# Attention projections 512 columns wide, and the next group's projection between the head pairs

## The chip, the core and the metric

The kernel runs on one core of one Trainium2 chip. The metric is device time in microseconds (us). The engines are named as in the profile: PE is TensorE (matrix products; PEld is its loading of the stationary operand), DVE is VectorE, ACT is ScalarE, POOL is GpSimd, and SP is SyncE, whose queue issues most transfers.

## The reference

The program is one inference step of a two-layer encoder trunk for 640 tokens: a prompt of 512 and 8 running streams of 16. Layer 0 is a mixer (spatial gating and a gated convolution) and a feed-forward block; layer 1 is forgetting attention and a feed-forward block. The change is in the attention. Cut to it:

```
z = rmsnorm(x) @ w_in                        # 1024 -> 3 x 1024 + 16
q, k, v, f = split(z)                        # 16 heads of 64
q, k = rmsnorm(q, q_norm), rmsnorm(k, k_norm)       # per head
logf = log_sigmoid(f + b_f);  d = cumsum(logf)
s = q k^T / 8 + d_query - d_key,  later keys masked
o = softmax(s) v                             # streams: 256 cached keys ahead of their own 16
x = x + o @ w_out;   k, v and logf are outputs too
```

All of it is float32. The kernel splits each float32 operand into two float32r parts (hi and lo) and forms hi x hi, lo x hi and hi x lo, so a product of the reference is three matrix products here.

## The kernel before

Tokens are in five blocks of 128, the last of which holds the streams; the 1024 features are eight chunks (h[0] to h[7], each a hi and a lo tile: hh, hl). The 16 heads are four groups of four heads, and a group is two pairs of heads.

**Projection.** `project` (L484 to L524) makes queries, keys and values of one group, one kind after the other. A kind is 256 columns wide. Its weights come as two tiles of 128 x 1024 from DRAM, by `weights` (L77): a landing tile `raw`, and `whi` and `wlo`, which ACT (L88) and DVE (L89) write. All three have three buffers. For each block of tokens 8 chunks x 3 products go into half a PSUM bank of `pj` (two banks); the activations are stationary and 256 columns of the weights move (L507). ACT evacuates each block (L510); for queries and keys ACT squares (L515), DVE sums by head (L516), POOL takes the root (L152), and DVE multiplies (L519, L521 for the keys). Keys and values leave for DRAM on ACT's queue (L523).

**Attention of a group.** `stream_operands` (L597; its transposes are L602) transposes the streams' queries and keys. `operands` (L529) builds the operands of a pair: transposes on PE (L537), evacuated and split by ACT and DVE (L544 to L549), with parts copied to other partitions by transfers on SP's queue (qa to qa, L545; ka to kb, L548; decay sums from DRAM, L551 and L552). `prompt_block` takes 128 queries of one head: two products for the scores (L569, L570) into one of two `sc` banks, mask and maximum on DVE, exponential on ACT, reciprocal and scaling on DVE, transposes of the probabilities (L576), evacuation to `u` (L579, L581), and the product with the values (L583, `pv`). `streams_pair` does the same for two streams (L634 to L670).

**Order.** The loop at L743 says for each group: project, then operands of the first pair, then for each pair the steps "b30", "s0", "b31", "o", ... where b30 is block 3 of head 0 of the pair, s0 is a stream step, and "o" in the first pair makes the second pair's operands. The tile framework then orders each engine's instructions by a schedule of its own, in which an instruction that comes earlier in the program goes first where both can run. So products of the next group's projection stand between the attention products of the present one. The decay sums (`decay`, L413) are made between queries and keys of group 0: forget logits (`pf`), their logarithms, running sums, and a way through DRAM. Behind group 3, the output projection over the chunks of groups 0 to 2 (`po`, L764 to L774, using the `pj` banks) is what remains to stand between.

## Time and profile before

| | us |
|---|---|
| time, median of 3 runs | 1533.71 (1533.48 to 1533.86) |
| profiled execution, span from the first to the last instruction | 1531.9 |
| PE busy in it | 1517.8 |
| DVE busy | 899.1 |
| ACT busy | 559.4 |
| POOL busy | 237.4 |

The profiled execution has no time of its own beside its span; the median of the runs is 1.8 us longer than the span. A busy time is the sum over which an engine had an instruction under way; products on PE overlap, so their spacing is read from the chain of waits, which gives, in order of time, pieces of "start, length, engine, tile, line, count". In the groups of instructions, "x480 | 137.7, 287" means 480 instructions, 137.7 us busy, 287 ns from start to end of one. A timeline row is "start, length, engine, line, operation, out<-in".

### The profile page before, as it was taken

Reading aid. Unit: us, or ns where it says so; the run is one execution under the profiler, and the core shown is the slowest. Engines: PE = TensorE matmul, PEld = TensorE weight load, DVE = VectorE, ACT = ScalarE, POOL = GpSimd, SP = SyncE. Lnnn points to the kernel's source line nnn. Section 1 sums busy time; section 2 is a strip of 40 time slices with the busy share of each in tenths; the row PEclk is TensorE's granted clock in tenths of the full one; section 3 lists DMA queues with packets and bytes.
Section 4 is the critical chain, followed back from the end, with each engine's and each line's share of the span. In section 5 each row is a group of like instructions: output and inputs, shape, how many; then the busy total and the mean of one; then the engine's idle time right before and its main releaser. Section 6 shows DMA issues by size and latency. Waiting matters only on the chain.

```text
span 1531.9 us, 26648 instructions
## 1 busy us (share of the span) xinstructions
PE 1517.8 (99%) x11008; PEld 1473.5 (96%) x11008; DVE 899.1 (59%) x1541; ACT 559.4 (37%) x918; POOL 237.4 (15%) x281
## 2 busy tenths in 40 slices
PE   8999999999999999999999999999999999999999
PEld 6999999999999999999989888888999999999998
DVE  6545437644653655675676766768765466365463
ACT  5422334322322322345545454535432233133231
POOL 5000122201210201143111111003221021021010
PEclk9999999999999999999999999999999999999999
DMA  6222212222223222243544343523222222321313
GB/s 226 77 82 73 77 56 85 68 81 85 62 64 95 64 66 93 62 156 103 180 128 136 122 123 104 183 60 107 83 60 76 87 67 57 98 73 53 107 47 106
DMA packets 52296, 142.90 MB, mean 93 GB/s; under 512 B 6656, under 2 KB 13744, under 8 KB 52048
## 3 DMA queue, kind: packets, MB, share of 16 engines
q1 hardware_dynamic: 45424, 133.79, 28.6%
q10 hardware_dynamic: 6752, 7.41, 1.4%
q8 instruction: 87, 1.43, 0.4%
q14 instruction: 33, 0.27, 0.1%
HBM read 125.41 MB, written 11.54 MB: 89 GB/s over the span
## 4 chain that ended last, share of the span: by engine, by line
PE 96%; DVE 2%; issue 1%; ACT 1%; DMA 0%; POOL 0%; SPq 0%; DVEq 0%; ACTq 0%
PE mm L109 71%; PE pj L507 10%; PE pv L583 3%; PE po L109 2%; PE pt L576 1%; PE mm L239 1%; PE pt L662 1%; PE sc L569 1%; DVE hl L132 1%; PE sc L570 1%; DVE wlo L89 1%; PE scs L641 1%; PE pt L537 1%; PE pt L655 0%; PE scs L634 0%
## 5 line engine op out<-in xcount | busy, mean ns | idle before, releaser
L88 ACT CAST whi<-raw 128x1024 fp32r<-128x1024 f32 (+4 forms) x222 | 207.6, 937 | 494.6 <-PE mm L109 426.1
L109 PE MATMUL mm<-hl,whi 128*128 128x320 f32 x1664 | 379.4, 309 | 0.5 <-DVE hl L132 0.5
L109 PE MATMUL mm<-hh,whi 128*128 128x320 f32 x1664 | 379.8, 309 | 0.0
L109 PE MATMUL mm<-hh,wlo 128*128 128x320 f32 x1664 | 379.2, 309 | 0.0
L109 PEld LDWEIGHTS mm<-hl,whi 128*128 128x128 f32 x1664 | 278.2, 188 | 0.7 <-DVE hl L132 0.7
L109 PEld LDWEIGHTS mm<-hh,whi 128*128 128x128 f32 x1664 | 278.2, 188 | 0.1
L109 PEld LDWEIGHTS mm<-hh,wlo 128*128 128x128 f32 x1664 | 278.0, 188 | 0.0
L89 DVE TENSOR_TENSOR wlo<-raw,whi 128x1024 fp32r<-128x1024 f32 (+4 forms) x222 | 245.5, 1107 | 33.3 <-ACT whi L88 33.0
L109 PE MATMUL mm<-sh,wlo 128*128 128x320 f32 x866 | 197.2, 309 | 1.3 <-DVE wlo L89 1.3
L109 PE MATMUL mm<-sl,whi 128*128 128x320 f32 x866 | 197.2, 309 | 0.0
L109 PE MATMUL mm<-sh,whi 128*128 128x320 f32 x866 | 196.2, 309 | 0.0
L202 POOL COPY so<-zp 128x18 f32<-128x18 f32 x88 | 89.4, 1016 | 570.4 <-DVE zp L191 570.4
L190 DVE TENSOR_TENSOR zp<-mm,rb 128x512 f32<-128x512 f32 x88 | 60.9, 692 | 195.8 <-PE mm L109 195.8
L209 DVE TENSOR_TENSOR x<-mm,x 128x640 f32<-128x640 f32 x79 | 65.0, 823 | 185.6 <-PE mm L109 185.6
L198 DVE SCALAR_TENSOR_TENSOR t<-zp,cst,t 128x656 f32<-128x656 f32 x184 | 165.1, 900 | 10.3 <-ACT t L196 5.6
L109 PEld LDWEIGHTS mm<-sh,wlo 128*128 128x128 f32 x866 | 144.6, 188 | 1.6 <-DVE wlo L89 1.6
L109 PEld LDWEIGHTS mm<-sl,whi 128*128 128x128 f32 x866 | 144.8, 188 | 0.0
L109 PEld LDWEIGHTS mm<-sh,whi 128*128 128x128 f32 x866 | 144.4, 188 | 0.2 <-issue 0.2
L507 PE MATMUL pj<-wlo,hh 128*128 128x256 f32 x480 | 137.7, 287 | 0.7 <-DVE wlo L89 0.7
L507 PE MATMUL pj<-whi,hh 128*128 128x256 f32 x480 | 137.7, 287 | 0.0
L507 PE MATMUL pj<-whi,hl 128*128 128x256 f32 x480 | 137.5, 287 | 0.0
L507 PEld LDWEIGHTS pj<-wlo,hh 128*128 128x128 f32 x480 | 91.6, 191 | 2.8 <-issue 1.6
(188 smaller groups left out, 1691.3 us busy)
## 6 DMA issues: line engine op xcount, KB each, us to landing
raw<-w_up SPq DMA_DIRECT2D x88, 512.0 KB
raw<-w_dn SPq DMA_DIRECT2D x32, 384.0 KB
raw<-w_c SPq DMA_DIRECT2D x24, 512.0 KB
raw<-w_dn SPq DMA_DIRECT2D x32, 320.0 KB
raw<-w_ab SPq DMA_DIRECT2D x16, 512.0 KB
ck<-c_k SPq DMA_DIRECT2D x16, 512.0 KB
cv<-c_v SPq DMA_DIRECT2D x16, 512.0 KB
o_kv<-z ACTq DMA_DIRECT2D x8, 640.0 KB
```

Of the source, the lines that this page charges most:

```text
L88: nc.scalar.copy(out=hi[:, c], in_=raw[:, c])
L89: nc.vector.tensor_tensor(out=lo[:, c], in0=raw[:, c], in1=hi[:, c].bitcast(F32), op=ALU.subtract)
L109: nc.tensor.matmul(outs[h], lhsT=l, rhs=r[:, h * HT:(h + 1) * HT], start=start and k == 0, stop=stop and k == 2)
L132: nc.vector.scalar_tensor_tensor(out=lo, in0=x, scalar=gs, in1=hi.bitcast(F32), op0=ALU.mult, op1=ALU.subtract)
L190: nc.vector.tensor_tensor(out=op, in0=a[:, 0:TP], in1=b[:, 0:TP], op=ALU.mult)
L198: nc.vector.scalar_tensor_tensor(out=cv[:, 0:CW], in0=zp[:, i:i + CW], scalar=w[:, i:i + 1], in1=cv[:, 0:CW], op0=ALU.mult, op1=ALU.add)
L202: self.nc.gpsimd.tensor_copy(out=out.rearrange("p (s c) -> p s c", c=2), in_=zp[:, 496:ZW].rearrange("p (s c) -> p s c", c=18)[:, :, 16:18])
L209: self.nc.vector.tensor_tensor(out=x, in0=ps[:, C0:C0 + T], in1=x, op=ALU.add)
L239: nc.tensor.matmul(pvs[tb], lhsT=l[:, tb * P:(tb + 1) * P], rhs=r[:, (kc % 2) * 512:(kc % 2 + 1) * 512], start=kc == 0 and k == 0, stop=kc ...
L507: nc.tensor.matmul(out[tb], lhsT=l[:, tb * P:(tb + 1) * P], rhs=r[:, c:c + 256], start=kc == 0 and i == 0, stop=kc == 7 and i == 2)
L537: nc.tensor.transpose(t[:, tb * P:(tb + 1) * P], z[i][:, tb, pair * P:(pair + 1) * P], k.ident)
L583: nc.tensor.matmul(ov[64 * hh:64 * hh + 64, i * P:n], lhsT=z[2][:, j, (2 * pair + hh) * 64:(2 * pair + hh) * 64 + 64], rhs=u[:, j * P:(j + ...
```

## The change

The weights of queries and keys of a group stand side by side in DRAM (`w_qk`, 512 columns), and so do the values of two groups (`w_vc`). `project` is replaced by `walk`, `project_qk` (one group) and `project_v` (two groups). Each product is 512 columns wide and fills a whole `pj` bank; a projection holds four weight tiles, and a block of tokens is evacuated, squared and normed when its walk is done. `whi` and `wlo` have four buffers, `raw` keeps three. In group 0 the queries and keys are projected, then the decay sums are made, then the values of groups 0 and 1 are projected. Queries and keys of group g+1 are projected at step "o" of the first pair of group g; the values of groups 2 and 3 at step "o" of the second pair of group 0. The remaining lines of the diff take comments out, lay out the weights in DRAM, and set a smaller scratch area for transfers that this kernel doesn't issue.

```diff
-        self.wp = pool(ctx, "wts", bufs=3)
+        self.wp = pool(ctx, "wts", bufs=4)
...
-        raw = self.wp.tile([P, 1024], F32, tag="raw", name=self.nm("raw"))
+        raw = self.wp.tile([P, 1024], F32, tag="raw", name=self.nm("raw"), bufs=3)
...
-    def project(self, g, h, first, after_q=None):
...
+    def walk(self, us, n, h, pairs):
+
+        k, nc = self.k, self.nc
+        out = [None] * 5
+        for tbs in ([(0, 1), (2, 3), (4,)] if pairs else [(tb,) for tb in range(5)]):
+            for tb in tbs:
+                out[tb] = self.pj.tile([P, 512], F32, tag="pj", name=k.nm("pj"))
+            for kc in range(8):
+                wh, wl = us[kc // n]
+                hh, hl = h[kc]
+                c = (kc % n) * 512
+                for tb in tbs:
+                    for i, (l, r) in enumerate(((hh, wh), (hl, wh), (hh, wl))):
+                        nc.tensor.matmul(out[tb], lhsT=l[:, tb * P:(tb + 1) * P], rhs=r[:, c:c + 512],
+                                         start=kc == 0 and i == 0, stop=kc == 7 and i == 2)
+            for tb in tbs:
+                yield tb, out[tb]
+
+    def project_qk(self, g, h):
+
+        k, nc, io = self.k, self.nc, self.io
+        us = [k.weights(io["w_qk"][g, u]) for u in range(4)]
+        zt = self.zp.tile([P, 5, 512], F32, tag="qk", name=k.nm("z"), bufs=2)
+        ss = self.zp.tile([P, 40], F32, tag="ss", name=k.nm("ss"))
+        for tb, o in self.walk(us, 2, h, g == 0):
+            nc.scalar.activation(out=zt[:, tb, :], in_=o, func=AF.Copy, scale=self.rt[:, tb:tb + 1])
+            sq = self.zp.tile([P, 512], F32, tag="sq", name=k.nm("sq"), bufs=1)
+            nc.scalar.activation(out=sq, in_=zt[:, tb, :], func=AF.Square)
+            s = ss[:, tb * 8:tb * 8 + 8]
+            nc.vector.reduce_sum(out=s, in_=sq.rearrange("p (h d) -> p h d", d=64), axis=AX.X)
+            k.rstd_of(s, s, 1.0 / 64)
...
+    def project_v(self, gg, h):
+
+        k, nc, io = self.k, self.nc, self.io
+        us = [k.weights(io["w_vc"][gg, u]) for u in range(4)]
+        zt = self.zp.tile([P, 5, 512], F32, tag="v", name=k.nm("z"), bufs=2)
+        for tb, o in self.walk(us, 2, h, False):
+            nc.scalar.activation(out=zt[:, tb, :], in_=o, func=AF.Copy, scale=self.rt[:, tb:tb + 1])
...
+    qk, v = at.project_qk(0, h), []
+    decay()
+    v += at.project_v(0, h)
     for g in range(4):
-        z = at.project(g, h, g == 0, decay if g == 0 else None)
+        z = qk + (v[g],)
...
                 if st == "o":
                     if pair == 0:
                         pops[1] = at.operands(g, 1, z)
+                        if g < 3:
+                            qk = at.project_qk(g + 1, h)
+                    elif g == 0:
+                        v += at.project_v(1, h)
```

The schedule follows. In the rows below a row is an instruction on PE in its order: line, operation, out<-in, size, and a count where equal ones follow each other. z are the projected queries, keys or values, pt a PSUM tile of transposes, p and u probabilities before and after their transposition, pp and pn those of the streams, on the streams' results, ka, kb, qa and qb the operands of a pair. Lines of the new kernel are six higher in the attention (L543 is the transpose of the operands, L575 and L576 are the scores).

The start of group 2 on PE, before: the operands' transposes, with the last products of the group ahead between them, and then products of the projection.

```order
L583 MATMUL pv_8406<-u_8636,z_7941 64x128
L537 MATMUL pt_9153<-cst,z_8668 128x128
L583 MATMUL pv_8406<-u_8652,z_7941 64x128
L537 MATMUL pt_9153<-cst,z_8668 128x128 x3
L537 MATMUL pt_9158<-cst,z_8836 128x128 x4
L507 MATMUL pj_9734<-whi_9728,hl_6173 128x256
L507 MATMUL pj_9734<-wlo_9729,hh_6172 128x256
```

The same place in the change:

```order
L543 MATMUL pt_8601<-cst,z_8009 128x128 x4
L589 MATMUL pv_8334<-u_8580,z_6742 64x128
L543 MATMUL pt_8606<-cst,z_8009 128x128 x4
L109 MATMUL po_9976<-sh_9373,whi_9971 128x320
L109 MATMUL po_9977<-sh_9373,whi_9971 128x320
L575 MATMUL sc_8636<-ka_8612,qa_8611 128x512
L640 MATMUL scs_8662<-sr,sl 128x272
```

Before, a run of projection products followed the transposes; now two products of the output projection stand between the transposes and the first score.

The second pair of group 2 on PE, before:

```order
L583 MATMUL pv_9187<-u_9329,z_9006 64x128 x3
L655 MATMUL pt_9357<-cst,pp_9349 128x128 x2
L655 MATMUL pt_9357<-cst,pn_6351 128x128
L569 MATMUL sc_9454<-ka_9176,qa_9175 128x128
L570 MATMUL sc_9454<-kb_9178,qb_9177 128x128
L507 MATMUL pj_9903<-whi_9890,hh_6080 128x256
L507 MATMUL pj_9903<-whi_9890,hl_6081 128x256
```

And in the change:

```order
L589 MATMUL pv_8635<-u_8969,z_7518 64x128 x3
L661 MATMUL pt_8997<-cst,pp_8989 128x128 x2
L661 MATMUL pt_8997<-cst,pn_6351 128x128
L575 MATMUL sc_9060<-ka_8624,qa_8623 128x256
L576 MATMUL sc_9060<-kb_8626,qb_8625 128x256
L575 MATMUL sc_9078<-ka_8612,qa_8611 128x128
L576 MATMUL sc_9078<-kb_8614,qb_8613 128x128
L668 MATMUL pt_8997<-cv_8976,up_9001 32x128 x8
L668 MATMUL pt_8997<-z_7518,up_9001 32x128 x4
L582 MATMUL pt_9033<-cst,p_9026 128x128 x3
```

The projection's products are gone from this place, and attention products follow each other.

53 lines of the change are left out of this document (13 added, 40 removed).

## The prediction

> **What bounds the kernel now.** I read the page's engine shares first, then the chain of waits, then the busy times by stage, then TensorE's waits.
>
> ```profile
> span 1531.9 us, 26648 instructions
> PE 1517.8 (99%) x11008; PEld 1473.5 (96%) x11008; DVE 899.1 (59%) x1541; ACT 559.4 (37%) x918; POOL 237.4 (15%) x281
> PE 96%; DVE 2%; issue 1%; ACT 1%; DMA 0%; POOL 0%; SPq 0%; DVEq 0%; ACTq 0%
> ```
>
> TensorE is busy 99% of the span and is 96% of the chain that ended last. So the time is the number of products times their spacing, plus the few waits. The attention stage runs from 680 to about 1040 us, and the busy times show it closed as well (columns: length, then PE, PEld, DVE, ACT, POOL, granted clock, DMA share, GB/s):
>
> ```profile
> 723.00:806.00 83.00, 83.00 (x776) 75.52 (x775) 56.07 (x158) 40.02 (x100) 11.07 (x11) 1.00 0.46 146
> 806.00:886.00 80.00, 80.00 (x727) 70.48 (x726) 52.52 (x151) 39.16 (x98) 10.21 (x10) 1.00 0.39 124
> 886.00:965.00 79.00, 79.00 (x719) 69.49 (x717) 53.47 (x153) 38.85 (x101) 10.04 (x10) 1.00 0.37 116
> 965.00:1040.00 75.00, 74.40 (x617) 63.67 (x616) 53.73 (x152) 32.59 (x85) 0.27 (x4) 1.00 0.38 117
> 1030.60:1039.10 8.50, 7.90 (x75) 5.82 (x74) 6.39 (x25) 3.72 (x13) 0.00 (x0) 1.00 0.09 33
> 1034.00:1039.20 5.20, 4.60 (x50) 3.10 (x42) 3.62 (x15) 2.34 (x9) 0.00 (x0) 1.00 0.04 13
> ```
>
> The first three rows are groups 0 to 2. The softmax of a group has long chains over DVE and ACT, yet TensorE never idles in them, because projection products of the next group stand between the attention's own. The fifth row is the one place where nothing fills in, the end of group 3: there TensorE is idle 0.60 of 8.50 us, 7%; in the second half of it (last row) 0.60 of 5.20, 12%. All TensorE waits of this stage are small:
>
> ```profile
> PE mm L109 <- DVE wlo L89: 1.3, 1, 1.3
> PE pj L507 <- DVE wlo L89: 0.7, 1, 0.7
> PE pv L583 <- ACT u L581: 0.4, 1, 0.4
> PE pv L583 <- DVE u L579: 0.2, 1, 0.2
> ```
>
> **Part 1, wider products.** 1440 products of 256 columns (three groups like the first row below) become 720 of 512. Their spacing comes from the chain, which gives runs without a gap:
>
> ```profile
> L507 PE MATMUL pj<-whi,hh 128*128 128x256 f32 x480 | 137.7, 287 | 0.0
> 679.94 5.52 PE pj L507 x46
> 227.19 452.76 PE mm L109 x3087
> 20.40 2.72 PE mm L239 x12
> ```
>
> 256 columns: 5.52/46 = 120 ns. 320 columns: 452.76/3087 = 146.7. 512 columns (the first mixer has them): 2.72/12 = 226.7. A column costs (226.7 - 120)/256 = 0.417 ns, and every product 13.3 ns whatever its width. So 1440 x 120 = 172.8 us becomes 720 x 226.7 = 163.2: **-9.6 us**. I allow 0.3 either way, since three widths lie on one line. It is all on the path, since TensorE bounds the stage. The Trainium skill, "TensorE: Matmul & The Clock Gate", section "Back-to-back issue gap", gives an isolated warm spacing of N/2.4 + 2.5 ns, and by it part 1 would save only 720 x 2.5 = 1.8 us (an estimate from that page). This trace differs: 13.3 ns, at all three widths.
>
> **Part 2, fewer pieces.** A projection that resumes after another kind of work starts slowly:
>
> ```profile
> 686.33 0.37 PE L507 MATMUL pj<-whi,hl 128*128 128x256 f32 x1
> 686.54 0.28 PE L507 MATMUL pj<-wlo,hh 128*128 128x256 f32 x1
> ```
>
> Start to start 0.21 us instead of 0.12: 0.09 for the change. In the built order, pieces of projection (pj, po) fall from 138 to 71; that is 67 x 0.09 = 6.0 us at most, and nothing at least if the change is paid anyway between two attention products. Changes between full products and those of 64 or 32 columns or fewer rows fall from 313 to 286; I take 27 x 0.09 = **-2.4 us**.
>
> **Part 3, the fill is spent early.** This is the price. Before, the next group's projection stood behind a group's attention in the program, so it was left over for every gap. Now queries and keys of group g+1 stand in the middle of group g's first pair, and the values of groups 2 and 3 in group 0. In the new order the last projection product stands before the end of group 1. Group 2 keeps 60 output-projection products (60 x 146.7 ns = 8.8 us) and group 3 keeps 174 (25.5 us); po can't start more, since chunks 4 and 5 are only complete when group 2 ends, and two PSUM tiles hold it.
>
> A group's attention alone is 79.0 - 360 x 0.12 = 35.8 us of TensorE (third window). The stretches without fill, in proportion to their products, are about 18 us (end of group 1: 79 rows of the order), 31 us (end of group 2: 126 rows) and, in group 3, 12.5 instead of 8.5. DVE isn't far behind there:
>
> ```profile
> L89 DVE TENSOR_TENSOR wlo<-raw,whi 128x1024 fp32r<-128x1024 f32 x24 | 29.3, 1221 | 11.3 <-ACT whi L88 11.2
> L516 DVE TENSOR_REDUCE ss<-sq 128x4 f32<-128x256 f32 x40 | 15.9, 412 | 14.2 <-ACT sq L515 14.1
> L519 DVE TENSOR_TENSOR z<-z,ss 128x1280 f32<-128x1280 f32 x8 | 11.9, 1490 | 1.9 <-POOL ss L152 1.6
> L151 DVE TENSOR_SCALAR ss<-ss 128x4 f32<-128x4 f32 x40 | 6.3, 164 | 0.2
> L521 DVE TENSOR_TENSOR z<-z,atcst 128x1280 f32<-128x1280 f32 x4 | 5.9, 1486 | 0.1
> ```
>
> Of 53.5 us of DVE in the third window the projection has 6 x 1.22 + 10 x 0.41 + 2 x 1.49 + 10 x 0.16 + 1.49: 17.5. That leaves 36 of DVE for 35.8 of TensorE, level. So each wait on the other may show, but neither is overrun. I take the 7% of the measured stretch: (18 + 31 + 4) x 0.07 = **+3.7 us**; below 0, above its 12%: 6.4.
>
> **Part 4, the group starts.** A group's first score needs its operands: transposes, ACT, DVE, and copies between partitions by DMA on SP's queue. The third group start of the trace (group 2):
>
> ```profile
> 890.67 6.82 PE pj L507 x57
> 889.68 0.98 PE L537 MATMUL pt<-cst,z 128*128 128x128 f32 x7
> 891.11 0.53 SPq L545 DMA_DIRECT2D qa<-qa  x1
> 891.73 0.55 SPq L548 DMA_DIRECT2D kb<-ka  x1
> 897.33 0.40 PE L569 MATMUL sc<-ka,qa 128*128 128x512 f32 x1
> 726.68 0.61 SPq L482 DMA_DIRECT2D sl<-sr  x1
> 728.61 0.68 ACT L544 ACTIVATE qa<-pt,qn 64x512 fp32r<-64x512 f32 x1 [2.34 <-DMA sl<-sr]
> ```
>
> Transposes end at 890.66, the score comes at 897.33, and 57 projection products (6.82 us) stand between. The last two rows show a small copy landing 1.9 us after its issue, so the score's operand was there between 891.11 + 1.9 = 893.0 and 897.33: 2.3 to 6.7 us after the transposes. In the new order groups 2 and 3 have only two po products there (0.3 us); what stands behind the score on TensorE, the streams' scores and po, waits with it, and DVE and ACT with those. Each start costs 2.0 to 6.4; the large loads ahead on SP's queue (ck, cv, x) speak for neither end, so I take the middle, 4.2, and **+8.4 us** for two (4.0 to 12.8). Group 1's start keeps 28 wide products (6.3 us) and costs nothing; without them it would cost the same 4.2.
>
> **Part 5, the first group.** The decay chain now starts after queries and keys.
>
> ```profile
> 702.05 0.46 PE L109 MATMUL pf<-hh,wlo 128*128 128x320 f32 x2
> L569 PE MATMUL sc<-ka,qa x64: 222/365/503, 738.9 to 1033.4; 128*128 128x512 f32 x16, 128*128 128x384 f32 x16, 128*128 128x256 f32 x16, 128*128 128x128 f32 x16
> L88 ACT CAST whi<-raw 128x1024 fp32r<-128x1024 f32 x23 | 24.0, 1045 | 11.5 <-PE pj L507 7.8 <-issue 1.8 <-PE pf L109 1.5
> 2.58 4.82 DMA x<-xT
> ```
>
> The forget product ends near 702.3 and the first score is at 738.9: 36.6 us. In the new order 148 wide products and 12 transposes (0.98/7 = 0.14 each at most) cover it: 33.6 + 1.7 = 35.3, 1.3 short. But the score at 738.9 may have been ready earlier: **+0.8** (0 to 3). A projection now holds four weight tiles, all that there are. In its last block of tokens (24 products, 5.4 us) the first is free after 1.4, split by ACT (1.05) and DVE (1.22) at 3.6: in time. The fourth waits for a landing buffer, free at 3.6; with a load as long as the start's (last row, 4.8) it is ready at 10.7, wanted at 9.5. **+1.2** where values of group 0 meet group 1's keys with no attention between (0 to 3). The extra split buffer may remove the 1.3 us wait behind the stage: **-0.6** (0 to -1.3). The narrower evacuations, squares and norms on ACT, DVE and POOL become half as many and wider; they lie beside TensorE and count as nothing, and so do the stores of keys and values. Were DVE not covered, a group's 17.5 us of them would show.
>
> **Sum:** -9.6 - 2.4 + 3.7 + 8.4 + 0.8 + 1.2 - 0.6 = +1.5 us. The profiled span is 1531.9, the timed median 1533.7, so 1.8 us lie around the span: 1531.9 + 1.5 + 1.8 = **1535 us**, no change that a measurement of this kernel tells (that takes 0.2%, 3.1 us).
>
> **Rivals.**
> - *The waits stay small.* Operands land soon after issue and the stretches run full: only the lower ends are paid, -12.6 + 4.0 = -8.6, **1525**. For it: the trace's unfilled stretch is 93% busy. Against it: nothing in the trace shows an operand before 897.
> - *The group starts and unfilled stretches decide.* Slower: two starts at 6.4 and the stretches at 12%, that is 12.8 + 6.4 + 2.0 - 0.6 - 12.0 = +8.6, and each start's drain of the last softmax at its 0.6 (fifth window) on top of it: +9.8, **1543**. It decides once the two together pass 12 us. For it: there is no fill at those places in the order. Against it: fill was plenty before, so 6.8 us say little of what was needed.
> - *The weights decide.* All three later projections are late too: 3 x 1.2 more, and the first one at 3.0: +6.9, **1541**. Against it: attention products stand between.
> - *The clock falls.* If TensorE's clock halves after each of the two waits for as long as the wait lasted (4.2 us), 2 x 2.1 is added: +5.7, **1539**. The windows above all grant 1.00, but hold no such wait. The Trainium skill, "TensorE: Matmul & The Clock Gate", section "What's actually happening", has this gate with an idle window of some 3.4 us; no run here shows it yet.
> - *The width saves nothing.* The fixed 13.3 ns stays as 26.7 per wide product: +9.6 on the sum, **1545**. The 512-column row speaks against it.
>
> **How the numbers follow.** The forecast (1531 to 1539 by its own costs) has 0.42: of it 0.04 lies below 1530.6, 0.27 within 0.2%, 0.11 above. Small waits 0.33, all faster. Starts and stretches 0.15, weights 0.05, clock 0.03, width 0.02: 0.25, all slower. So faster 0.37, within 0.2% 0.27, slower 0.36. The range 1523 to 1545 goes 2 us beyond the outer rivals and leaves out about 1 in 10 on each side, for scheduling that none of this prices.
>
> **What would show it.** Wide projection products 0.227 us apart (part 1). A TensorE wait of 2 to 6 us before the first score of groups 2 and 3, and none before group 1's (part 4). Idle shares near 7% in the ends of groups 1 and 2 (part 3). The wait on wlo within 3 us (part 5). The prediction is wrong if the stage shortens by more than 8 us or if waits outside these places appear.

## The result, and the profile after

The changed kernel is slower: 1542.6 us (1542.1 to 1547.5, four executions) against 1533.8 (1533.5 to 1535.8) of the kernel before on the same chip. The ratio is 1.0062, with a 95% interval of 1.0047 to 1.0077. The forecast was 1535, no change; the measured 8.8 us more lie inside the range given, and beyond the 0.2% that a measurement of this kernel can tell.

The page of the changed kernel, profiled in an execution of 1547.5 us (span, the engines' busy times, the clock granted in 40 slices, the chain by engine):

```profile
span 1545.7 us, 25114 instructions
PE 1518.9 (98%) x10288; PEld 1437.5 (93%) x10288; DVE 897.0 (58%) x1529; ACT 554.6 (36%) x868; POOL 230.2 (15%) x261
PEclk9999999999999999999999998899999999999999
PE 95%; DVE 3%; ACT 1%; issue 1%; DMA 0%; POOL 0%; SPq 0%; DVEq 0%; ACTq 0%
```

PE has 720 instructions fewer and is still busy for as long (1518.9 us, 1517.8 before), in a span that is 13.8 us longer. Two slices, from about 927 to 1005 us, have an 8 in the clock's row: there TensorE ran for a part of the time at half clock, which the kernel before did nowhere in the attention. What PE waited for in the attention and just behind it:

```profile
PE po L109 <- ACT sh L97: 6.1, 2, 3.0
PE pv L589 <- DVE u L585: 2.6, 3, 1.1
PE pv L589 <- ACT u L587: 1.3, 3, 0.7
PE mm L109 <- DVE hl L132: 1.1, 1, 1.1
PE pj L497 <- ACT z L509: 0.9, 1, 0.9
```

Before, one row of the attention reached 0.7 us. The first row here is two waits of 3.0 us, from 926.8 and from 986.2: the starts of groups 2 and 3. The chain of waits (start, length, what) shows the first of them, and above it the wide products that cover the first group:

```profile
728.97 16.36 PE pj L497 x72
...
925.90 0.68 ACT qa L550
926.58 0.47 ACT x L567
...
928.08 0.36 ACT qbd L615
928.46 0.59 ACT ka L553
929.07 0.73 ACT sh L97
...
929.84 0.56 PE po L109 x2
```

A wide product takes 16.36/72 = 0.227 us. And at the start of group 2 the chain runs through ACT alone for 3.9 us, one evacuation after another, while PE, from 926.8 on, has nothing to do.

The busy times by stretch (length, then PE, PEld, DVE, ACT, POOL, granted clock, DMA share, GB/s) show what this does to the clock:

```profile
927.68:931.09 3.41, 1.25 (x16) 0.83 (x20) 1.92 (x3) 3.19 (x7) 0.00 (x0) 1.00 0.38 89
931.09:934.50 3.41, 3.41 (x24) 2.18 (x12) 2.54 (x7) 0.83 (x1) 0.00 (x0) 0.50 0.49 100
951.57:954.99 3.42, 2.15 (x34) 1.51 (x33) 3.29 (x10) 2.53 (x7) 0.00 (x0) 1.00 0.37 83
954.99:972.05 17.06, 16.63 (x86) 10.00 (x89) 9.48 (x36) 5.04 (x17) 0.00 (x0) 0.50 0.20 67
985.70:989.12 3.42, 0.47 (x4) 0.23 (x3) 1.43 (x2) 3.33 (x8) 0.00 (x0) 1.00 0.18 41
989.12:995.95 6.83, 6.76 (x33) 4.77 (x34) 5.02 (x10) 2.07 (x5) 0.00 (x0) 0.50 0.64 184
1047.10:1053.90 6.80, 4.72 (x32) 3.39 (x32) 4.96 (x22) 3.22 (x13) 0.00 (x0) 1.00 0.00 0
```

The trace's records of the clock say 0.50 in three stretches, of 3.41, 17.06 and 6.83 us: one, five and two windows of 3.413. Each begins right behind a window in which PE was busy 1.25, 2.15 and 0.47 of 3.4 us. 27.3 us of the attention ran at half rate.

To set the kernels beside each other, the attention stage (first pj product to the first product behind the attention) is divided up. For each product the time to the next product's start is compared with (columns + 32)/2400 us, which is the 13.3 ns and 0.417 ns a column read from three widths of the trace before. "Products" is the sum of these prices, so it follows from the products' number and width; "half clock" is what products in half-clock stretches took beyond that price, up to twice; "waits" the excesses above 0.3 us that are left; "rest" the small differences that remain. Where exactly the line of 0.3 us is drawn in the half-clock stretches moves up to 0.7 us of a row between waits and rest. All in us, from the profiled execution; time, ratio to the kernel before (95% interval) and mean granted clock from the timed ones.

```
                             time    ratio (interval)         clock       stage  products  waits  half clock  rest
before                       1533.8  1                        1.000       359.3  323.5      1.9   0.0        33.8
after                        1542.6  1.0062 (1.0047, 1.0077)  .991-.996   373.9  313.9     19.7   8.6        31.7
place undone                 1543.9  1.0068 (1.0050, 1.0086)  .990-.995   372.6  313.9     17.3   8.5        32.8
narrow, between pairs        1556.7  1.0151 (1.0136, 1.0166)  .992-.994   381.0  323.5     18.3   4.9        34.3
products added in blocks     1552.1  1.0120 (1.0103, 1.0137)  .996-.997   378.4  328.2     15.7   3.9        30.6
products added in the wait   1540.4  1.0040 (1.0025, 1.0055)  .994-.999   364.1  319.4     13.3   0.2        31.3
paced                        1553.3  1.0128 (1.0113, 1.0143)  .991-.992   378.7  313.9     24.1   7.3        33.4
values narrow                1544.8  1.0067 (1.0051, 1.0083)  .996-1.000  370.1  317.1     15.8   2.9        34.2
one buffer for q and k       1551.9  1.0111 (1.0094, 1.0128)  .992-.993   375.7  317.1     20.4   4.7        33.4
block held for the start     1560.6  1.0165 (1.0150, 1.0181)  .990-.992   384.3  313.9     30.7   6.6        33.1
operands early               1539.6  1.0039 (1.0026, 1.0051)  .994-.999   364.0  313.9     12.2   1.3        36.6
paced, operands early        1544.3  1.0065 (1.0050, 1.0080)  .992-.997   369.7  313.9     17.3   4.7        33.8
operands earlier             1530.4  0.9974 (0.9963, 0.9986)  .994-.999   354.0  313.9      7.8   2.1        30.1
narrow, operands earlier     1540.8  1.0043 (1.0026, 1.0059)  .999-1.000  366.6  323.5      6.5   1.0        35.6
```

Before and after differ by -9.6 in products, -2.1 in the rest, +17.8 in waits and +8.6 at half clock: +14.6 in the stage of the profiled executions. The other three executions of the changed kernel had a mean clock of 0.995 or 0.996 instead of 0.991 and were 4.5 to 5.4 us shorter, which is why the median shows 8.8.

### The profile page after: what moved, and what is told of

It reads as the page before. It is cut to its first block, busy times and chain, and to the rows that moved or that the text cites. A ratio compares the mean times of both kernels' runs of the same rounds, so it can differ in the third digit from the quotient of the medians.

```text
span 1545.7 us, 25114 instructions
## 1 busy us (share of the span) xinstructions
PE 1518.9 (98%) x10288; PEld 1437.5 (93%) x10288; DVE 897.0 (58%) x1529; ACT 554.6 (36%) x868; POOL 230.2 (15%) x261
## 4 chain that ended last, share of the span: by engine, by line
PE 95%; DVE 3%; ACT 1%; issue 1%; DMA 0%; POOL 0%; SPq 0%; DVEq 0%; ACTq 0%
PE mm L109 71%; PE pj L497 11%; PE po L109 3%; PE pv L589 2%; PE pt L582 1%; PE mm L239 1%; PE sc L575 1%; PE pt L668 1%; DVE wlo L89 1%; PE sc L576 1%; PE scs L647 1%; DVE hl L132 1%; PE pf L109 0%; PE pt L543 0%; PE scs L640 0%
## 5 line engine op out<-in xcount | busy, mean ns | idle before, releaser
L497 PE MATMUL pj<-whi,hh 128*128 128x512 f32 x240 | 95.2, 397 | 1.0 <-ACT z L509 0.9
L497 PE MATMUL pj<-whi,hl 128*128 128x512 f32 x240 | 94.3, 393 | 0.0
L497 PE MATMUL pj<-wlo,hh 128*128 128x512 f32 x240 | 93.7, 394 | 0.0
L196 ACT ACTIVATE t<-zp,cst 128x656 f32<-128x656 f32 x92 | 77.6, 845 | 36.3 <-DVE zp L191 36.3
```

Source lines behind the costliest of these rows:

```text
L196: nc.scalar.activation(out=cv[:, 0:CW], in_=zp[:, 2:ZW], func=AF.Copy, scale=w[:, 2:3])
L497: nc.tensor.matmul(out[tb], lhsT=l[:, tb * P:(tb + 1) * P], rhs=r[:, c:c + 512], start=kc == 0 and i == 0, stop=kc == 7 and i == 2)
```

## The experiments

**The place undone.** Is it the place between the pairs that costs?

```diff
     for g in range(4):
+        if g:
+            qk = at.project_qk(g, h)
+        if g == 2:
+            v += at.project_v(1, h)
         z = qk + (v[g],)
...
-                        if g < 3:
-                            qk = at.project_qk(g + 1, h)
-                    elif g == 0:
-                        v += at.project_v(1, h)
```

> The 512-column products and their buffers stay; only the place in the program goes back: queries with keys of a group at that group's start, the values of groups 2 and 3 at the start of group 2. Theory of buffers and order (the projection runs as early as its buffers let it, wherever it is written, because the order on TensorE is made by readiness): no change against the changed kernel, 1540 to 1545 us, unfilled stretches of the attention in group 2, and a mean granted clock of 0.99 to 0.996. Rival, the place between the pairs is what costs: the time falls back to the kernel before less what the width gives, 1522 to 1534 us, with a granted clock of 1.000.

Measured 1543.9 us, against 1542.6 of the change: the same.

```profile
PE po L109 <- ACT sh L97: 5.6, 2, 3.0
```

The two waits are there too, 2.6 and 3.0 us, at a mean clock of 0.991 in the profiled execution, and the half-clock stretches are at the same places (931.08 to 934.50, 954.98 to 972.04, 989.11 to 995.94). With the projection written at the start of its own group the schedule still runs it ahead, as far as its two wide buffers let it. Between these two places it makes no difference for the wide kernel.

**Narrow products between the pairs.** The place alone, with the products, buffers and weight tiles of the kernel before.

```diff
+    zn = at.project(0, h, True, decay)
     for g in range(4):
-        z = at.project(g, h, g == 0, decay if g == 0 else None)
+        z = zn
...
                         pops[1] = at.operands(g, 1, z)
+                        if g < 3:
+                            zn = at.project(g + 1, h, False)
```

> The 256-column products, z tiles and weight tiles of the kernel before; only the place moves: the whole projection of group g+1 is written between the head pairs of group g. Theory of buffers and order: the three z buffers of 256 columns hold the projection back nearly as before, so 1532 to 1537 us, granted clock 0.998 or more. Rival, the place itself costs: 1539 to 1545 us, with waits of 2 to 6 us ahead of the groups or a clock of 0.996 or less.

Measured 1556.7 us, longer than either expectation: slower than the wide kernel with the same place by 14 us, and than the kernel before by 23. The theory that the buffers alone hold the projection back falls. The timeline of PE at the start of group 1 (start, length, line, what, and in brackets the idle time ahead):

```profile
841.58 0.66 PE L537 MATMUL pt<-cst,z 128*128 128x128 f32 x4
844.77 0.69 PE L569 MATMUL sc<-ka,qa 128*128 128x512 f32 x1 [2.54 <-DVE ka L549]
...
847.03 0.80 PE L570 MATMUL sc<-kb,qb 68*128 68x512 f32 x1
849.75 0.79 PE L569 MATMUL sc<-ka,qa 128*128 128x512 f32 x1 [1.93 <-ACT p L591]
```

Now all three starts are bare, and the first head's and the second head's scores wait one after the other: 2.7 and 2.5 us (excess over the price) at group 1, 2.2 at group 2, 3.2 at group 3. In the kernel before, 57 projection products stood at the like place of group 2, because part of the group's own projection was left over. The four waits make 10.7 of the 18.3 us of waits here. So what costs most is that nothing is left for the start, whichever part of the change does it. It also sets the two widths beside each other with the place held equal (buffers and weight tiles differ too): the wide kernel's products come to 9.6 us less by their price, and it is 14 us faster.

**Products added in the blocks.** 63 products of 128x512, which nobody reads, behind the softmax of blocks in group 2 and of the last blocks of groups 1 and 2.

```diff
         self.softmax(p_, s[:, 0:n], True)
+        for _ in range(extra):      # 3 in most blocks of group 2, 12 in the last block of groups 1 and 2
+            nc.tensor.matmul(s, lhsT=h[0][0][:, 0:P], rhs=h[0][0][:, 0:512], start=True, stop=True)
         t = self.ptile()
```

> The changed kernel with work added and none left out: 63 products of 128x512 whose result nobody reads (63 x 0.227 = 14.3 us of TensorE) behind the softmax of the last 12 blocks but some of group 2 (3 each) and of the last blocks of groups 1 and 2 (12 each), where the changed kernel's waits lie and where its clock was halved. Theory of the clock (the changed kernel loses some 6 to 14 us to stretches at half clock, and these come from TensorE doing too little): the mean granted clock is 1.000 or 0.999, 6 to 8 us come back, of the 14.3 us added some 8 to 12 fall into waits, and the time is 1537 to 1543 us: not longer than the changed kernel's in spite of the work added. Rival, the waits cost and the halved clock falls into them: the added products fill waits, but nothing comes back; 1543 to 1557 us. A rival of chance (the clock drops for another reason): clock still 0.991 to 0.996.

Measured 1552.1 us at a clock of 0.996 to 0.997, a time in the range of the first rival. The clock did rise (half clock costs 3.9 us instead of 8.6), and the stretch of 17 us at half rate in the middle of group 2 is gone:

```profile
951.57:972.05 20.48, 18.62 (x145) 12.78 (x146) 15.13 (x50) 8.34 (x25) 0.00 (x0) 1.00 0.29 95
929.50:932.94 3.44, 0.87 (x4) 0.60 (x4) 1.63 (x4) 3.33 (x8) 0.00 (x0) 1.00 0.32 73
932.94:939.77 6.83, 6.83 (x36) 5.35 (x37) 4.79 (x11) 2.33 (x6) 0.00 (x0) 0.50 0.67 209
```

But the waits only fell from 19.7 to 15.7 us, so that some 10 of the 14.3 us added came on top. The expectation that 8 to 12 of them would fall into waits was wrong. The likely reason is that the products stand ahead of the probabilities' transposes on PE and push the softmax's chain back; that wasn't measured apart. At the group starts the 12 products ran before the wait, not in it, and the clock still fell behind it (second and third row). In group 2 the clock answered to how little TensorE does; filling by itself isn't free.

**Products added inside the wait.** The same at the two starts only, and so that the products lie in the wait: the first of them needs the first operand of the new group.

```diff
+        for c in range(extra):      # 12 in the first block of groups 2 and 3
+            l, r = (qa[0:64, 0:P], qa[0:64]) if c == 0 else (h[0][0][:, 0:P], h[0][0][:, 0:512])
+            nc.tensor.matmul(s, lhsT=l, rhs=r, start=True, stop=True)
         nc.tensor.matmul(s[:, 0:n], lhsT=qa[:, i * P:n], ...
```

> The changed kernel with 12 products of 128x512 added (2.7 us) at the starts of groups 2 and 3, whose result nobody reads; the first of them needs the first operand of the new group, so that they lie inside the wait of 3.2 us and not before it. Nothing else moves. Theory of the clock (an idle stretch at the start halves the clock for one or two windows of 3.4 us right after it): the waits at these starts fall under 1 us, the time is not longer by the added work, the halved windows after the starts vanish and only those of the unfilled stretch in group 2 stay; mean granted clock 0.996 to 0.998, 1537 to 1541 us. Rival, the halved windows after the starts have another cause: clock as before (0.991 to 0.996), 1541 to 1547 us. Rival, products in a wait push the scores back: 1545 us or more with clock 0.996 to 0.998.

Measured 1540.4 us (1538.6 to 1543.0), clock 0.994 to 0.999: with 5.4 us of useless work added, 2.2 us less than the change at the medians. The intervals of the two ratios overlap, so what is shown is that the added work cost nothing; that it saves time isn't. Timeline of PE, then windows:

```profile
926.66 2.79 PE L577 MATMUL sc<-hh 128*128 128x512 f32 x11
929.39 0.39 PE L643 MATMUL scs<-sr,sl 18*128 18x272 f32 x1
930.34 0.56 PE L109 MATMUL po<-sh,whi 128*128 128x320 f32 x2
```

```profile
931.09:934.50 3.41, 2.89 (x20) 2.53 (x19) 3.35 (x8) 0.83 (x1) 0.00 (x0) 1.00 0.74 196
954.99:972.05 17.06, 15.81 (x168) 11.15 (x166) 13.83 (x50) 7.94 (x25) 0.00 (x0) 1.00 0.38 119
```

The streams' score starts at 929.39 (930.57 in the change; the schedule has moved it ahead of the output projection's products), the window behind the start keeps full clock, and in this execution the stretch from 955 to 972 does too, though nothing was added there. The stage of this execution, the fastest of its four, is 9.8 us shorter than that of the change's profiled one, the slowest of its four: 8.4 of it at half clock, 6.4 in waits, less 5.5 of products. Within this kernel the four executions read 1538.6, 1539.5, 1541.3 and 1543.0 us at 0.999, 0.998, 0.997 and 0.994: about 0.9 us for each 0.001 of mean clock. At that rate the change's 1542.2 at 0.995 would be some 1538 at full clock. So, by this estimate, half clock is about half of the 8.8 us, and waits less the width's gain are the other half.

**Paced.** 512 wide, but spread out: a block of 128 tokens after every few steps, held by its evacuation's scale, which waits for a softmax.

```diff
+    def gate(self, tb):
...
+        g = self.zp.tile([P, 1], F32, tag="gate", name=k.nm("gate"), bufs=4)
+        nc.vector.scalar_tensor_tensor(out=g, in0=self.l, scalar=0.0, in1=self.rt[:, tb:tb + 1], op0=ALU.mult, op1=ALU.add)
...
-            nc.scalar.activation(out=zt[:, tb, :], in_=o, func=AF.Copy, scale=self.rt[:, tb:tb + 1])
+            rt = self.gate(tb) if g else self.rt[:, tb:tb + 1]
+            nc.scalar.activation(out=zt[:, tb, :], in_=o, func=AF.Copy, scale=rt)
```

> 512 columns, buffers and weight tiles as in the change, but the projection is paced: one block of 128 tokens after every few steps of the attention, held there by the scale of its evacuation, which is now written by an operation that reads the softmax before it (0 times that sum plus the scale). 20 tiny operations are added, no work is left out. Theory (the width itself gives 9.6 us in products and 2.4 in pieces; the loss comes from the fill spent early, through waits and a halved clock): no stretch of the attention without fill but the last, clock 1.000, 1521 to 1528 us. Rival, the width gives nothing here, or its cost lies elsewhere: 1531 to 1536 us at clock 1.000. Rival, the pacing is no cure: 1538 to 1545 us, clock below 0.997.

Measured 1553.3 us at 0.991: longer than all three expectations, though, counted in its products, only the last of its stretches without fill is long.

```profile
PE sc L586 <- ACT p L608: 5.3, 3, 1.9
PE sc L586 <- DVE qb L563: 5.3, 2, 3.8
PE po L109 <- ACT sh L97: 3.0, 1, 3.0
```

The waits are at the starts again, now of groups 1, 2 and 3: 1.7 and 2.2, 4.0 and 2.5, and 3.2 us, with half-clock windows behind each. Spreading the fill over the group leaves none for its start. Of its 24.1 us of waits 13.6 are at the starts (6.5 of 19.7 in the change), so where fill is missing counted for more here than how much of the attention is without it. What the pacing costs by itself this run doesn't separate.

**Three ways to hold something for the start.** Values again 256 columns and one group at a time, in one buffer; the same with one buffer for queries and keys and two for the values; and the paced kernel with the last 128 tokens of the queries and keys held until the group ends.

```diff
-        zt = self.zp.tile([P, 5, 512], F32, tag="v", name=k.nm("z"), bufs=2)     # values narrow
+        zt = self.zp.tile([P, 5, 256], F32, tag="v", name=k.nm("z"), bufs=1)
...
-        zt = self.zp.tile([P, 5, 512], F32, tag="qk", name=k.nm("z"), bufs=2)    # one buffer for q and k
+        zt = self.zp.tile([P, 5, 512], F32, tag="qk", name=k.nm("z"), bufs=1)
...
+            late = self.held(h) if hold and tbs == (4,) else None                # block held: a copy of
-                        nc.tensor.matmul(out[tb], lhsT=l[:, ...                  # h[0]'s last 128 tokens,
+                        nc.tensor.matmul(out[tb], lhsT=late if first else ...    # made after a softmax
```

> Only the queries with keys stay 512 columns wide; the values are again 256 columns, one group at a time, written at that group's start, into one buffer (the kernel before had two), so that they cannot run before the group ahead of them has ended and stand on TensorE where the operands of the new group are being formed. Queries with keys are written at the group's start too. Theory of the uncovered starts (a group's start costs about 3 us of waiting and then some microseconds at half clock when no projection is left for it): no wait above 2 us at a start, granted clock 1.000, and the width saves 480 x (2 x 0.120 - 0.227) = 6.4 us in products, 1 to 2 in pieces, less 1 to 3 for stretches without fill: 1526 to 1530 us, faster than both kernels. Rival, the width gives nothing even with the starts covered: 1532 to 1536 us at clock 1.000. Rival, something else in the wide queries with keys costs (their four weight tiles, their pieces): 1538 us or more.

> As the kernel with narrow values, but held back at the other place: one buffer for the wide queries with keys instead of two, two buffers for the narrow values (as before the change). The queries with keys of the next group can then start only when the second pair's operands have been taken, and the values of the group stand at its start. Theory of the uncovered starts: again no wait above 2 us at a start; 8 us of the attention without fill at the end of each of three groups instead of one stretch of 13: clock 1.000, 1526 to 1531 us. Rival, what decides is the amount of attention without fill, not the starts: 3 x 8.3 against 12.9 + 5.6 + 6.1 is the same sum, so the same time as the kernel with narrow values within 1 us, whatever that is. Rival, a buffer too few makes the operands wait: 1536 us or more with waits of TensorE on the evacuation of the queries.

> All 512 wide and paced as the paced kernel, but the last 128 tokens of the next group's queries with keys (24 products, 24 x 0.227 = 5.4 us, which the new group's first scores do not need) are held for the group's start: their first product takes a copy of its 128 x 128 operand that is made, unchanged, after the last softmax but few. Theory of the uncovered starts: the waits at the starts of groups 1 and 3 fall from some 4 and 3 us to under 1; that of group 2 partly (the order leaves 1.4 us of products there); two stretches of 15 us without fill at the ends of groups 0 and 2 may halve the clock once or twice; 1528 to 1540 us, and in any case under the paced kernel's 1553 by 10 us or more. Rival, the paced kernel loses by the pacing itself (evacuations that wait for a softmax): 1545 us or more.

Measured 1544.8, 1551.9 and 1560.6 us: all three fail, each in the range of the last rival of its expectation, and each in its own way. The first is the change's time within the noise, the others are longer than it. Rows of their waits, one kernel after the other:

```profile
PE pj L535 <- ACT z L538: 4.2, 3, 1.6
PE sc L585 <- DMA qa<-qa: 2.2, 1, 2.2
```

```profile
PE sc L585 <- ACT p L607: 5.6, 4, 1.9
PE pj L497 <- ACT z L509: 2.8, 3, 0.9
```

```profile
PE sc L597 <- ACT p L619: 6.5, 5, 1.9
PE sc L597 <- DVE ka L577: 4.0, 2, 2.3
```

With narrow values the products held for the start wait themselves: their PSUM bank is free only when ACT has evacuated the blocks before, and those go into the buffer that the old values have just left. ACT then has four evacuations more in the very chain that the start is waiting for:

```profile
806.76 0.57 ACT L577 COPY x<-pv 128x512 f32<-128x512 f32 x1
807.22 1.55 ACT L538 ACTIVATE z<-pj,rt 128x256 f32<-128x256 f32 x4
808.66 1.50 ACT L625 ACTIVATE qbd<-pt,qn 64x128 f32<-64x128 f32 x4
810.18 0.58 ACT L563 CAST ka<-pt 64x512 fp32r<-64x512 f32 x1
```

Its clock was 0.996 to 1.000, so that half clock explains little of its time; the waits (15.8 us in the stage) do. With one buffer for queries and keys, and with the held block, products do run at the starts, but not between the first two heads' scores, and scores at the starts still wait, 1.6 to 2.5 us each: four times with one buffer, five times with the held block. In the held kernel, moreover, nothing can pass the held block, so that the ends of two groups stand without fill: 30.7 us of waits, the most of all. The rival of the second expectation, that only the amount without fill counts, falls with them: by it the first two would be equal, and they are 7 us apart.

**Operands early.** Instead of covering the start, take it away: the operand chain of the next group's first pair and streams is written into the end of the group before. The wide projection has the queries and keys ready by then.

```diff
-        sops = at.stream_operands(g, z)
-        at.streams_start(g)
+        if g == 0:
+            sops = at.stream_operands(0, z)
+            at.streams_start(0)
+            first = at.operands(0, 0, z)
...
-                pops = [at.operands(g, 0, z), None]
+                pops = [first, None]
...
+                if pair == 1 and g < 3 and st == "b10":      # "s1" in the kernel with operands earlier
+                    zn = qk + (None,)
+                    nsops = at.stream_operands(g + 1, zn)
+                    at.streams_start(g + 1)
+                    first = at.operands(g + 1, 0, zn)
...
```

> The changed kernel with one thing moved: the operands of the next group's first pair and of its streams, with the rows loaded for the streams, are written after the sixth prompt block of the second pair, not at the start of the next group; the queries and keys that they need are there by then, since the wide projection runs ahead. No work is added or left out. Theory of the uncovered starts (a start costs the 3.2 us wait on the operand chain, some 0.5 us behind it, and the halved windows after it): no wait above 2 us at the starts of groups 2 and 3, clock 0.997 or more; against the changed kernel's 1542 that is 2 x 3.7 = 7 us less waiting and 2 to 5 us of clock: 1531 to 1537 us. Rival, ScalarE and VectorE have no room in the last blocks, so that the chain's 3 us come back as waits of the softmax: 1540 to 1544 us.

> The paced kernel (one block of 128 tokens of the projection after every few steps, held by its evacuation's scale) with the operands of the next group's first pair and streams written after the sixth prompt block of the second pair. No stretch of the attention above 5.5 us is then without products between its steps. Theory (the paced kernel's loss of 20 us was 14.5 us of waits at three starts and 2 us of clock behind each): no wait above 2 us at a start, clock 0.998 or more, 1526 to 1534 us. Rival, pacing by the evacuation costs by itself (scores wait for a bank while the products stand in line before them): 1537 to 1545 us. If the width is worth its 9.6 us at all, this or the kernel with operands early must come under 1533.

> As the kernel with operands early, but written already after the last pair of streams of the second pair, three prompt blocks sooner; the stretches without fill get shorter at the ends of groups 1 and 2 (6.3 and 14.2 us instead of 6.8 and 17.1) and come about behind the starts instead (5.5 and 6.4 us). Theory of the uncovered starts: the same as there within 2 us, 1530 to 1537 us, clock 0.997 or more. Rival, the earlier place pushes the softmax of four blocks back by ScalarE's 4 us at each of three groups: 3 to 8 us more than there.

Measured 1539.6 (operands early), 1544.3 (paced as well) and 1530.4 us (operands earlier). The first is above its range and just under its rival's. By the second expectation's own test, that one of the first two must come under 1533 if the width is worth its price, the width failed; the third kernel and the next experiment bring it back. In the last one the waits of PE on this chain, and the clock:

```profile
core 0: 1527.6 us, clock 0.997
PE pt L543 <- ACT qbd L615: 1.2, 2, 0.9
PE sc L575 <- ACT p L597: 0.9, 1, 0.9
PE po L109 <- ACT sh L97: 0.7, 1, 0.7
```

No wait at a start is above 1.2 us any more. At 0.9974 of the kernel before (0.9963 to 0.9986) it is the one version that beats both kernels, by 3.4 us and by some 12. The earlier place is also better than the later one by 9 us, where the theory said within 2: 4.4 of that is in waits above 0.3 us, 6.5 in small differences between products, which I can't break down further. The kernel with the later place still waited 1.6 us at both starts, for the same ACT row:

```profile
PE po L109 <- ACT sh L97: 2.9, 2, 1.4
```

The paced kernel gains 9 us by the early operands, but stays 5 us behind the unpaced one, with 17.3 us of waits for 12.2. The largest row of its attention is scores that wait:

```profile
PE sc L586 <- ACT p L608: 4.5, 3, 1.5
```

Its time is in the range of the rival by which pacing by the evacuation costs by itself.

**Narrow products with operands earlier.** The width alone, on top of the best version.

```diff
+                if pair == 1 and g < 3 and st == "s1":
+                    nsops = at.stream_operands(g + 1, zn)
+                    at.streams_start(g + 1)
+                    first = at.operands(g + 1, 0, zn)
```

(on the kernel with narrow products between the pairs)

> The kernel with 256-column products between the pairs, with the operands of the next group's first pair and streams written after the last pair of streams, as in the kernel with operands earlier: it differs from that one in the width (and its buffers and weight tiles) alone. Theory (the width is worth its 9.6 us in products and 2.4 in pieces wherever the waits are the same, and the early operands are worth about 12 us to either width): 1540 to 1545 us. Rival, the early operands are all that made the kernel with operands earlier fast, and the width adds nothing to it: 1529 to 1533 us. Rival, the narrow kernel keeps its waits of 2.7 us at the starts, because its keys come too late for operands taken early: 1549 us or more.

Measured 1540.8 us (1539.9 to 1541.1) at 0.999 to 1.000; 10.4 us slower than the wide one with the operands at the same place, as forecast. In the stages of the profiled executions the wide one is 12.6 us shorter: 9.6 by its products' price, 5.5 in the rest, less 1.3 of waits and 1.1 at half clock. The width is worth its price here, and the operands' place is worth 12 us to the wide kernel and 16 to the narrow one.

## Why the prediction was wrong where it was

**Part 1, right.** The wide products are 0.227 us apart, and at that spacing the products of the stage sum to 9.6 us less. What is measured apart from that price is the comparison of widths with the operands earlier, 10.4 us at the medians; that it lies so near 9.6 is in part luck, since the rest differs by 5.5 there and waits and clock go the other way. The rival that the width saves nothing falls. With it goes, as the price of these products, the 2.5 ns of the Trainium skill, "TensorE: Matmul & The Clock Gate", section "Back-to-back issue gap": the 13.3 ns of the trace held.

**Part 2, about right.** The small differences fell by 2.1 us; -2.4 was taken. That may be luck: among the kernels with the same wide products the rest runs from 30.1 to 36.6.

**Part 4, right in size, wrong in its chain.** Waits of 3.2 us at the starts of groups 2 and 3, none at group 1's, where 28 wide products stood: 6.5 us for 8.4. But the step said that the score waits for copies by DMA. The chain of waits goes through ACT only: five kinds of evacuation and split, 3.9 us. PE stood at two products of the output projection, which wait for the last of the five (`sh`, ready at 929.79); the first score's own `ka` was finished by DVE at 929.75, so without those two products the start would have come no sooner to speak of:

```profile
929.07 0.68 DVE L555 TENSOR_TENSOR ka<-pt,ka 64x512 fp32r<-64x512 f32 x1 [1.71 <-ACT ka L553]
```

The prediction's words that nothing in the trace before shows an operand before 897 overlooked the same row there:

```profile
891.89 0.69 DVE L549 TENSOR_TENSOR ka<-pt,ka 64x512 fp32r<-64x512 f32 x1
```

It ends at 892.58, 1.9 us behind the transposes; in the change the same `ka` is done 2.9 us behind them, with ACT's pieces for the streams (`qbd`) in between. A copy does hold a score elsewhere: 2.2 us on qa<-qa in the kernel with narrow values. The ACT chain also said what to do: move it, not the transfers.

**Part 3, the term that was mis-sized.** It took 7% of the unfilled stretches, +3.7 us, with 6.4 as the upper end. Measured are 19.7 us of waits, less 6.5 of the starts, 1.1 at a place not foreseen and 1.9 that were there before: 10.2. The waits lie where the step put them: 2.1 us at the end of group 1, 6.0 in group 2 from 947 to 984, 2.7 at the end of group 3 (1.1 of that was there before). The 7% is about what the end of group 1 shows, where PE was idle 1.52 of 19.20 us (8%); it was 1.99 of 8.99 (22%) from 946 to 955 and 2.14 of 7.60 (28%) from 1046 on:

```profile
905.00:924.20 19.20, 17.68 (x169) 13.16 (x170) 17.88 (x61) 10.73 (x31) 1.84 (x1) 1.00 0.61 207
946.00:954.99 8.99, 7.00 (x71) 5.61 (x70) 8.02 (x24) 5.29 (x15) 0.00 (x0) 1.00 0.49 142
1046.00:1053.60 7.60, 5.46 (x55) 3.75 (x54) 6.04 (x27) 3.85 (x13) 0.00 (x0) 1.00 0.01 2
```

The 7% was taken from the one unfilled stretch of the trace, of 8.5 us, whose second half already showed 12%. In a longer stretch the work in flight runs out, and a wait is paid in each block: from 951.57 to 954.99 PE was busy 2.15 of 3.42 us. A share read at the beginning of a stretch is no share for a stretch four times as long.

**The clock, named and priced too low.** It was a rival at 0.03, with 4.2 us: two falls, each as long as the wait before it. The profiled execution lost 8.6 us to it, the others, by their 4.5 to 5.4 us less, about 4. It was wrong on two counts. A fall lasts in windows of 3.413 us, here one, five and two, whatever the wait was. And the longest followed no long wait: in the 25 us before 972 no single wait is above 1 us, by all that the trace shows it is the sum of small ones, part 3's waits, that made TensorE too idle. The Trainium skill, "TensorE: Matmul & The Clock Gate", section "A second HAM failure mode: psum-queue depth-cycling", tells of a kernel whose TensorE idles for very short times between groups of products often enough that the clock goes back and forth; this trace agrees (2.15 of 3.42 us busy, then five windows at 0.50). I had weighed the section on idle windows alone.

**Part 5, not seen.** PE is busy 125.9 of the 126 us from 680 to 806, so neither the decay chain (+0.8) nor the weights (+1.2) cost anything. The wait on wlo behind the stage (1.3) went, and one on hl there grew from 0.5 to 1.1. A wait of 1.1 us (0.9 by the profile's row) up to 882, of the projection for ACT's evacuation of a bank, was not foreseen; by the prediction's own sign, no waits outside the places it names, it speaks against it.

**Sum.** In the stage: -9.6 - 2.1 + 10.2 + 6.5 + 1.1 + 8.6 = +14.7 (measured 14.6) in the profiled execution; with the other executions' clock some 4 to 5 less. The forecast differs by part 3 and the clock, which hang together: the unfilled stretches were taken for nearly full, and the longest stretch at half clock, 4.8 of the 8.6 us, lies in one of them; the other 3.7 follow the two waits at the starts. The forecast of no change was missed by 7.6 us; the range held. The rival "the group starts and unfilled stretches decide" was 1543, with 0.15; it had the size, but as starts of 6.4, which were 3.2, and without the clock; that it comes so near 1542.6 is luck.

What stays open: why the half-clock stretch in group 2 lasts five windows although PE is busy 16.63 of 17.06 us in it, while others end after one (in the kernel with products added in the wait the same microseconds run at full clock); and whether the starts would cost less with ACT's pieces in another order, which wasn't tried.

## What to carry to other kernels

Filler work between dependent steps has to be counted place by place, and the places that needed it most here are the starts of a group, where a serial chain on another engine has to run before the first product can; ask of every change that moves filler ahead what then stands there, and if nothing does, move the chain into the group before rather than hold filler back for it, which was tried in three ways here: one gained nothing, two lost 9 and 18 us. When TensorE is the bound, price idleness twice: once as the wait, once as the clock behind it, and price it from windows of 3.4 us, not from single waits. A saving in products is real only in the kernel whose waits stay the same: the same width was worth 10 us here, and the change around it lost 18.

## What the runs showed of the hardware

**The clock falls without an idle window.** The clock's records lie on a grid of 3.413 us. For each of the 14 profiled executions the stretch from 680 to 1064 us was cut on that execution's own grid, and PE's busy share in each window at full clock was set against the next window's clock. 29 times the next one was at half clock. In 28 of these PE had been busy 63% of the window or less (in one 68%), and all 20 windows below 54% were followed by half clock. From 54% to 68% it went both ways. In the kernel before, no window of the attention is under 85%. The change's windows above show both: 2.15 of 3.42 us (63%) from 951.57 was followed by half clock, 4.72 of 6.80 (69%, two windows) from 1047.10 was not.

**Useless work can be free.** 24 products that nobody reads, 5.4 us, placed inside two waits, did not make the kernel longer (1540.4 us for 1542.6, within the noise): they lie in the waits, and in the profiled execution the clock behind these stayed up.

**The same code varies with the clock.** Executions of one kernel differ by up to 5.8 us (values narrow, 1541.9 to 1547.7). In most kernels the longer ones have the lower clock (operands earlier: 1527.4 at 0.999 to 1532.9 at 0.994; end to end 0.9 to 1.1 us for each 0.001 of mean granted clock there and with products added in the wait), but not strictly: with values narrow 1543.7 at 0.998 is shorter than 1545.8 at 0.999. The kernel before, with no window of the attention near the border, stays within 2.6 (1533.1 to 1535.8).
